# A decoder block on one core: the down projection with the tokens' operands as TensorE's weights

## The chip, the core and the metric

The kernel runs on one core of a Trainium2 chip. The metric is device microseconds per execution; the kernel before has a median of 1889.66 us over 3 runs (1889.62 to 1889.98). Five engines work side by side: TensorE (PE; its weight loads are shown apart as PEld), VectorE (DVE), ScalarE (ACT), GpSimd (POOL) and SyncE (SP), whose queue issues nearly all DMAs (SPq in the profile).

## The reference

One layer on 512 tokens of 2048 channels: RMSNorm, an input projection, three token mixers, an output projection with a residual, then a SwiGLU feed-forward layer of width 5632 with a second residual. The change concerns the last line, above all the product with `w_down`:

```python
x = x + mix @ w_out[l]
h2 = _rms_norm(x, norm2_g[l])
x = x + (jax.nn.silu(h2 @ w_gate[l]) * (h2 @ w_up[l])) @ w_down[l]
```

## The kernel before, in words

Arrays lie with channels on the 128 partitions and the 512 tokens on the free axis; the host turns the output back. Each fp32 operand is split into a high part rounded to fp32r and the rest (low part), and a product is three matmuls: high by high, high by low, low by high.

The stages in order: `in` (the first four tiles of the input projection, 16 steps k of 12 matmuls of 512 columns; lines 392 to 417), the other 26 tiles of the input projection with attention and convolution between them, the output projection, gate and up, and down. The rows of x and of w for the first steps are loaded by SP in the order of lines 288 to 292, ACT makes the high parts (`hh` L371, `wh` L245), DVE the low ones (`hl` L372, `wl` L232), and ten matmuls on a tile `idle` (L299) run ahead of the first one. `token_scale` sums squares over channels by matmuls with a column of ones (L322).

Gate/up and down use a Strassen-Winograd scheme: each block product is cut in 2 by 2 quarters and made of seven products q. The operands of the seven products are sums of quarters. For w these sums are made by POOL (`add` in `group`, L187); then ACT writes the high part twice, once to PSUM (`wn`, L251) and once to SBUF (`wh`, L252), and DVE subtracts to get the low part (`wl`, L232). `next_unit` hands out one such split unit of w at a time and splits two units ahead (`SPLIT_AHEAD`); three `wh` and three `wl` buffers exist. For the activations, ACT and DVE write tiles a (256 columns high, 256 low) in gate/up, which go to DRAM (`od`) and are loaded again in down.

Down in the kernel before: 25 blocks (table `DOWN`), each for two of the 16 tiles of 128 output channels and 5 to 8 of the 22 pairs of inner tiles. In `Block.multiply` (L1013) a 128x128 tile of w is TensorE's weights and the tokens move: `wh` by 512 columns (256 tokens high and low side by side), then `wl` by 256 columns (high alone). The sums have channels on partitions; unfinished ones go to DRAM (`yd`) and come back (`load_y`). `Down.done` adds PSUM to them on DVE (L1025, L1026; 128x256 each), the shared term u on POOL, and the residual x2 on POOL (L1147, L1148). `Down.store` writes 128x256 pieces to the output on SP (L1152), the last ones at once (`tail`).

Order is set by the program: `run(evacs)` issues what was put off ahead of each unit, `run(extras)` what was put off behind it; `later(n, ..., queue)` puts something off by n units. Each engine takes its instructions in that order, and SP takes DMAs in that order too.

Of the kernel before, what the change touches and what calls it, by code (L numbers as in the profile page):

```python
# [57 lines left out]
WARM = 10  # L58
# [12 lines left out]

GU_ORDER = [*range(1, 5), *range(6, NP), 0, 5]
STAY = (0, 5)


DOWN = [(0, 0, 5), (1, 0, 6), (2, 0, 7), (3, 1, 8), (4, 2, 9), (5, 3, 10), (6, 4, 11), (7, 5, 13),
        (0, 5, 12), (1, 6, 14), (2, 7, 15), (3, 8, 16), (4, 9, 17), (5, 10, 18), (6, 11, 19), (7, 13, 20),
        (0, 12, 17), (1, 14, 22), (2, 15, 22), (3, 16, 23), (4, 17, 24), (0, 17, 22), (5, 18, 25), (6, 19, 26), (7, 20, 27)]

FIRST = [min([w[1] for w in DOWN[t:]] + [99]) for t in range(len(DOWN) + 1)]  # L80
LAST = [max(w[2] for w in DOWN[:t + 1]) for t in range(len(DOWN))]
# [38 lines left out]
def kernel(ctx: ExitStack, tc: tile.TileContext, xT, wi, wo, wgu, wd, cst_in, outT):  # L120
# [27 lines left out]
    units = [wi[0][:, :T], wi[0][:, T:]] + [wi[u] for u in range(1, 2 * N_IN)]  # L148
# [19 lines left out]
    for u, unit in enumerate(units):  # L168
        entries.append((RAW_PLAIN[u % len(RAW_PLAIN)], u, [unit]))
        works.append((u, True, nc.vector))  # L170
# [33 lines left out]
    def down_block(n, half, first, end):  # L204

        parts = [(first, min(end, NP)), (0, end - NP)] if first < NP else [(first - NP, end - NP)]
        return [bass.AP(tensor=wd.tensor, offset=wd.offset + (n * P * NF + half * NP + a) * P,
                        ap=[[NF * P, P], [1, (b - a) * P]]) for a, b in parts if b > a]

    for t, (n, first, end) in enumerate(DOWN):  # L210
        group(f"d{t}", t % 2, (end - first) * P, {f"{i + 1}{k + 1}": down_block(n + 8 * i, k, first, end)
                                                  for i in range(2) for k in range(2)})
# [4 lines left out]
    def pump(limit):  # L217
        while at["entry"] < len(entries) and len(raws) < limit and entries[at["entry"]][0] not in held:
            buf, key, parts = entries[at["entry"]]
            t, o = take(buf, key, sum(p.shape[-1] for p in parts)), 0  # L220
# [15 lines left out]
    def split_up_to(i):  # L236
        while at["split"] <= min(i, len(works) - 1):
# [5 lines left out]
            if eng or "high" not in psum:  # L243
                eng = eng or nc.vector
                nc.scalar.copy(hi[:, :n], t[:, :n])  # L245
# [17 lines left out]
    def next_unit():  # L263
        sums_now()
        u = at["use"]
        at["use"] += 1
        lows_now()
        split_up_to(u + SPLIT_AHEAD)
        if not lows:
            pump(RAW_EARLY if u < 20 else RAW_BUFS)  # L270
        return splits.pop(u)
# [8 lines left out]
    nc.scalar.dma_start(cst, cst_in)  # L280
# [7 lines left out]
    for k in range(X_AHEAD):  # L288
        load_first(k)
        u = k if k < 2 else k // 2 + 1  # L290
        if u < RAW_EARLY and (k < 2 or k % 2 == 0):
            pump(u + 1)


    idle = slot("idle", BF16)
    nc.vector.memset(idle, 1.0)
    b = bank("idle")
    for i in range(WARM):
        nc.tensor.matmul(b, idle[:, :P], idle, start=True, stop=True)  # L299
# [10 lines left out]
    bones = cp.tile([P, 2], F32, name="bones")  # L310
    nc.vector.memset(bones, 0.0)
    nc.vector.memset(bones[0:HD, 0:1], 1.0)
    nc.vector.memset(bones[HD:P, 1:2], 1.0)
# [69 lines left out]
    def token_scale(acc, n, name, b=None):  # L383

        b = bank(name, NT) if b is None else b
        stat_rows(b[:, :, None], acc, ones)
        v, r = small(name + "v"), small(name + "r")
        nc.vector.tensor_scalar(v, b, 1.0 / n, EPS, op0=ALU.mult, op1=ALU.add)  # L388
# [5 lines left out]
    for k in range(2):  # L394
        h_hl[k] = scaled(xs[k], col(C_G1 + k), "h", k)
        split_up_to(k)
    pump(RAW_EARLY)
    add_square(ssum, xs[0], 0, "sq")
    for k in range(KT):

        if k == 0:
            h_hl[2] = scaled(xs[2], col(C_G1 + 2), "h", 2)
        if k < 2 or k % 2 == 0:
# [4 lines left out]
        if k and k + 2 < KT:  # L408
            h_hl[k + 2] = scaled(xs[k + 2], col(C_G1 + k + 2), "h", k + 2)
# [4 lines left out]
        h_lo.append(lo)  # L414
        for j in range(HEAD4):
            mm3(g4[j], wh[:, o:o + P], wl[:, o:o + P], hi, lo, k == 0, k == KT - 1)
            o += P
# [439 lines left out]
    x2d = {n: tc.dram_tile([P, T], F32, name=f"x2d{n}") for n in range(KT)}  # L857
# [15 lines left out]
    def scale_x2(n):  # L873
        j = n % NJ
        t = x2.pop(n)
        nc.sync.dma_start(x2d[n], t)
# [151 lines left out]
    class Wide(Block):  # L1028
# [55 lines left out]
        def piece(self, at, src):  # L1084
# [3 lines left out]
            for k in range(n):  # L1088
# [4 lines left out]
                if self.p in STAY:  # L1093
                    acts[q, self.p] = t
                if self.p not in STAY:
                    later(0, nc.sync.dma_start, od[self.p][:, (at + k) * T:(at + k + 1) * T], t.bitcast(F32),
                          queue=extras)
# [16 lines left out]
    y, yd = {}, {n: tc.dram_tile([P, T], F32, name=f"yd{n}") for n in range(KT)}  # L1114

    def visit(t):

        begin, last = [all(w[0] != DOWN[t][0] for w in part) for part in (DOWN[:t], DOWN[t + 1:])]

        return begin, last, t == 8 if DOWN[t][0] == 0 else last  # L1120

    def load_y(t):
        if t < len(DOWN):
            for n in (DOWN[t][0], DOWN[t][0] + 8):
                y[t, n] = slot(f"y{t}_{n}")
                if not visit(t)[0]:
                    nc.sync.dma_start(y[t, n], yd[n])
                if visit(t)[2]:
                    xr[n] = slot(f"yx{n}")
                    nc.sync.dma_start(xr[n], x2d[n])  # L1130

    class Down(Block):


        def __init__(self, t):
            super().__init__(f"d{t}", t % 2)
            self.n = DOWN[t][0]
            self.fresh, last, residual = visit(t)
            self.out = outT if last else yd
            self.tail = t == len(DOWN) - 1  # L1140
            self.y1, self.y2 = y.pop((t, self.n)), y.pop((t, self.n + 8))
            if residual:

                later(1, self.add_x2)

        def add_x2(self):
            nc.gpsimd.tensor_add(self.y2, self.y2, xr.pop(self.n + 8))  # L1147
            nc.gpsimd.tensor_add(self.y1, self.y1, xr.pop(self.n))  # L1148

        def store(self, n, t, cols):  # L1150
            def go():
                nc.sync.dma_start(self.out[n][:, cols], t[:, cols])  # L1152
            if self.tail:
                go()
            else:
                later(1, go, queue=extras)

        def done(self, q):
            one, two = slice(0, TH), slice(TH, T)
            if q == 1:  # L1160
                self.u = slot(f"{self.name}u")
                self.u1, self.u2 = halves(self.u)
                self.both(1, self.u1)
            elif q == 7:
                if self.fresh:
                    self.both(7, self.y2[:, two])
                else:
                    self.add(7, self.y2[:, two])
# [155 lines left out]
```

## Time and profile before

| | before |
|---|---|
| median of 3 runs | 1889.66 us (1889.62 to 1889.98) |
| the profiled execution | 1889.53 us, of it 1887.7 us span from the first to the last instruction |
| granted TensorE clock | 1.00 |
| PE busy; PEld busy | 1882.2 us; 1635.1 us |
| DVE, ACT, POOL busy | 1467.8, 1330.7, 996.4 us |
| DMA | 320.29 MB, mean 170 GB/s |

Busy time is the union of an engine's instructions. A matmul's own duration is longer than its distance to the next one, because matmuls are pipelined: how fast they go is read from the distance of their starts. A row of groups gives line, engine, operation, output<-inputs, shape, count, busy us, mean ns of one, and idle time ahead of it with what ended it. In a timeline the columns are start, duration, engine, line, operation, and in brackets the idle time before.

### The profile page before, as it was taken

How to read it: one execution, taken by the hardware profiler on the slowest of the kernel's cores; microseconds unless marked ns; L12 is line 12 of the kernel's file. 1: busy time of each engine (PE TensorE's matmuls, PEld its weight loads, DVE VectorE, ACT ScalarE, POOL GpSimd, SP SyncE). 2: the span in 40 equal slices, each digit the busy share in tenths (PEclk: the TensorE clock that was granted, in tenths of full speed). 3: DMA queues.
4: the chain of work that ended last, by engine and by line, in shares of the span. 5: the costliest groups of instructions: out<-in, count | busy, mean ns of one | idle time of the engine just before them, and what ended most of it. 6: DMA issues, size and time to landing. Idle time of an engine off the chain costs nothing.

```text
span 1887.7 us, 29650 instructions
## 1 busy us (share of the span) xinstructions
PE 1882.2 (100%) x10332; PEld 1635.1 (87%) x10332; DVE 1467.8 (78%) x2562; ACT 1330.7 (70%) x1856; POOL 996.4 (53%) x643
## 2 busy tenths in 40 slices
PE   9999999999999999999999999999999999999999
PEld 7888888888888888888888888888888888888888
DVE  6789978999679777777777777777787877677776
ACT  6356645453467887888888888888878877676775
POOL 0111011010003887877878878788767656565775
PEclk9999999999999999999999999999999999999999
DMA  7242242343343444454544545445447878777885
GB/s 269 86 126 86 81 123 88 112 118 122 124 144 105 142 147 153 139 181 152 164 144 146 177 141 167 140 160 167 146 159 248 272 261 275 256 260 232 306 272 196
DMA packets 136311, 320.29 MB, mean 170 GB/s; under 512 B 15585, under 2 KB 31073, under 8 KB 136161
## 3 DMA queue, kind: packets, MB, share of 16 engines
q1 hardware_dynamic: 136016, 318.31, 52.4%
q8 instruction: 81, 1.33, 0.3%
q14 instruction: 70, 0.57, 0.1%
q10 hardware_dynamic: 144, 0.10, 0.0%
HBM read 254.11 MB, written 55.84 MB: 164 GB/s over the span
## 4 chain that ended last, share of the span: by engine, by line
PE 99%; DMA 0%; SPq 0%; ACT 0%; DVE 0%; issue 0%; ACTq 0%; DVEq 0%
PE out L1013 68%; PE o L276 3%; PE o L274 3%; PE o L275 3%; PE cq L276 2%; PE cq L274 2%; PE cq L275 2%; PE av L274 1%; PE ak L274 1%; PE aq L274 1%; PE aq L276 1%; PE av L276 1%; PE ak L276 1%; PE av L275 1%; PE aq L275 1%; PE ak L275 1%
## 5 line engine op out<-in xcount | busy, mean ns | idle before, releaser
L1013 PE MATMUL out<-h,wh 128*128 128x512 f32 x2464 | 588.5, 391 | 0.0
L1013 PEld LDWEIGHTS out<-h,wh 128*128 128x128 f32 x2464 | 452.7, 188 | 87.5
L1013 PEld LDWEIGHTS out<-h,wl 128*128 128x128 f32 x2464 | 315.9, 191 | 12.0
L1013 PE MATMUL out<-h,wl 128*128 128x256 f32 x2464 | 319.6, 283 | 0.0
L1013 PE MATMUL out<-a,wh 128*128 128x512 f32 x1232 | 296.2, 391 | 0.0
L1013 PEld LDWEIGHTS out<-a,wh 128*128 128x128 f32 x1232 | 225.7, 188 | 43.5 <-ACT wh L252 0.4
L245 ACT CAST wh<-w 128x1024 fp32r<-128x1024 f32 (+1 forms) x93 | 96.8, 1041 | 122.4 <-PE o L275 51.6
L1013 PEld LDWEIGHTS out<-a,wl 128*128 128x128 f32 x1232 | 159.4, 191 | 6.9
L1013 PE MATMUL out<-a,wl 128*128 128x256 f32 x1232 | 161.5, 283 | 0.0
L232 DVE TENSOR_TENSOR wl<-w,wh 128x1024 fp32r<-128x1024 f32 (+1 forms) x93 | 112.5, 1209 | 39.4 <-ACT wh L245 39.3
L466 DVE SCALAR_TENSOR_TENSOR y<-bu,cst,y 128x511 f32<-128x511 f32 (+14 forms) x120 | 87.6, 730 | 0.4
L1025 DVE TENSOR_TENSOR y<-y,out 128x256 f32<-128x256 f32 x93 | 39.1, 421 | 46.0 <-PE out L1013 44.4
L274 PE MATMUL o<-mh_c,wh 128*128 128x512 f32 x128 | 51.1, 399 | 0.0
L274 PE MATMUL cq<-hh,wh 128*128 128x512 f32 x128 | 51.1, 399 | 0.0
L276 PE MATMUL cq<-hh,wl 128*128 128x512 f32 x128 | 50.0, 391 | 0.0
L276 PE MATMUL o<-mh_c,wl 128*128 128x512 f32 x128 | 50.0, 391 | 0.0
L275 PE MATMUL cq<-hl,wh 128*128 128x512 f32 x128 | 50.0, 390 | 0.0
L275 PE MATMUL o<-ml_c,wh 128*128 128x512 f32 x128 | 49.9, 390 | 0.0
L1026 DVE TENSOR_TENSOR y<-y,out 128x256 f32<-128x256 f32 x101 | 42.5, 421 | 3.5
L389 POOL TENSOR_TENSOR lvr<-lvv,nhalf 128x4 f32<-128x4 f32 x1 | 1.9, 1927 | 73.3 <-DVE lvv L388 73.3
L187 POOL TENSOR_TENSOR w('s', 'g1')_5687<-w('21', 'g1')_5533,w('22', 'g1')_5531 128x1024 f32<-128x1024 f32 x1 | 2.5, 2451 | 69.8 <-DVE wl L232 69.8
L868 DVE TENSOR_TENSOR xr<-xr,o 128x512 f32<-128x512 f32 x32 | 21.9, 683 | 13.6 <-PE o L276 12.8
(3137 smaller groups left out, 4868.9 us busy)
## 6 DMA issues: line engine op xcount, KB each, us to landing
a<-od SPq DMA_DIRECT2D x175, 256.0 KB, 5.0
od<-a SPq DMA_DIRECT2D x147, 256.0 KB, 4.6
w<-in_wi SPq DMA_DIRECT2D x59, 512.0 KB, 3.7
w<-in_wo SPq DMA_DIRECT2D x32, 512.0 KB, 3.6
yd<-y SPq DMA_DIRECT2D x68, 128.0 KB, 4.7
y<-yd SPq DMA_DIRECT2D x34, 256.0 KB, 4.8
x<-in_xT SPq DMA_DIRECT2D x16, 256.0 KB, 7.7
xr<-in_xT SPq DMA_DIRECT2D x16, 256.0 KB, 3.9
```

Of the source, the lines that this page charges most:

```text
L187: eng.tensor_add(out[:, :n], raws[key[a]][0][:, :n], raws[key[b]][0][:, :n])
L232: fn(*args)
L245: nc.scalar.copy(hi[:, :n], t[:, :n])
L274: nc.tensor.matmul(out, wh, xh, start=start, stop=False)
L275: nc.tensor.matmul(out, wh, xl, start=False, stop=False)
L276: nc.tensor.matmul(out, wl, xh, start=False, stop=stop)
L389: nc.gpsimd.tensor_tensor(r, v, nhalf[:, :NT], op=ALU.pow)
L466: nc.vector.scalar_tensor_tensor(yconv[j][:, i:], hconv[j][:, :T - i], c, yconv[j][:, i:], op0=ALU.mult, op1=ALU.add)
L868: nc.vector.tensor_add(t, t, b)
L1013: nc.tensor.matmul(out, lhs[:, s], rhs, start=begin, stop=x is xs[-1] and low == flip[0], skip_group_check=True)
L1025: sign(out, out if first is None else first, main)
L1026: sign(out, out, rest)
```

## The change

**Down.** The 16 sums of 128 tokens by 512 channels (key `(g, i, k, a)`: channel half i and 512 of its channels g, token half k and 128 of its tokens a) stay in SBUF from start to end, and start as x2. Down becomes 12 visits (`DOWN`): six ranges of pairs, 4, 3, 4, 3, 4 and 4 long, each for both g. A visit does the seven products in the order `D_ORDER`; a product has two units of w (A with two pairs, B with two or one, four channel tiles each) and two banks, one for each a. The tokens' tile (128 high or 128 low columns) is TensorE's weights, 512 columns of w move:

```diff
-                    out, lhs, rhs = (b[:, TH:], wl, x[:, :TH]) if low else (b, wh, x)
-                    nc.tensor.matmul(out, lhs[:, s], rhs, start=begin, ...
+        def multiply(self, q, b, units, a, lo, hi, start, stop):
+            high, low = slice(a * P, (a + 1) * P), slice(TH + a * P, TH + (a + 1) * P)
...
+                    nc.tensor.matmul(b[:, lo:hi], x[:, high], wh[:, s], start=start, ...
+                    nc.tensor.matmul(b[:, lo:hi], x[:, high], wl[:, s], start=False, ...
+                    nc.tensor.matmul(b[:, lo:hi], x[:, low], wh[:, s], start=False, ...
```

The split (`eng == "moves"`) copies with the tiles of a unit reordered, and the sums of w are four per unit kind on POOL: 21+11 (four units ahead), 21+22, +11, +12. A quarter of w is loaded in rows of 1 KB (two pairs) or 512 bytes (one).

```diff
+        for i, c in enumerate("AB"):
+            sums[base - 4 + i].append(add(c, "11", buf=bufs[c]["s"]))
+            sums[base + i].append(add(c, "22"))
+            sums[base + 3 + i].append(add(c, "11", last=True))
+            sums[base + 7 + i].append(add(c, "12"))
...
+                nc.scalar.copy(by(near), src)
+                nc.scalar.copy(by(hi), src)
+                nc.vector.tensor_sub(by(lo), src, by(near).bitcast(F32))
```

PSUM is added to the sums by `done`, mostly by DVE with 128x512 adds; q=1 goes by an ACT copy `u` to POOL:

```diff
+                if q == 7:
+                    self.add(1, 0, a, b, by)
+                    self.add(1, 1, a, b, by)
+                elif q == 1:
+                    nc.scalar.copy(self.u[a], b)
+                    later(a, self.add, 0, 0, a, self.u[a], nc.gpsimd)
+                elif q == 5:
+                    self.add(0, 1, a, b, by)
+                    self.add(1, 1, a, b, by, "tensor_sub")
+                elif q == 6:
+                    by.tensor_add(self.u[a], self.u[a], b)
...
```

behind q=6, six POOL adds of u follow in each visit.

**Turning.** x2 is read back in blocks of 32 by 32 during gate/up (from the fourth pair on, one key each), turned by a DVE transpose and stored as `x2t`. At the end `store` turns a sum and writes it with four DMAs of 32x16 runs of 32 floats:

```diff
+    def store(key, lo=0, hi=T, engs=(nc.sync,), now=False):
+        nc.vector.transpose(z[:, lo:hi], y[key][:, lo:hi])
+        def go():
+            for part in range(4):
+                to = out[c + lo:c + hi, 256 * k + P * a + 32 * part:256 * k + P * a + 32 * part + 32]
+                engs[part % len(engs)].dma_start(to.rearrange("(b i) t -> i b t", i=32), ...
+        if now:
+            go()
+        else:
+            later(1, go, queue=extras)
```

The eight sums of g=1 are stored during the last visit, one per unit. Of g=0, keys (1,1) and (1,0) are stored through `later` behind q=4 and q=2; (0,0) and (0,1) in the last product with `now=True`. That last product does a=0, then a=1 in two halves of 256 columns, and does not call `run(extras)`:

```diff
+            if tail:
+                for n, (a, lo, hi) in enumerate(((0, 0, T), (1, 0, TH), (1, TH, T))):
+                    self.multiply(q, out[n], units, a, lo, hi, True, True)
+                    nc.vector.tensor_add(s, s, out[n][:, lo:hi])
+                    store(key, lo, hi, (nc.sync, nc.scalar), now=True)
+                    if n == 0:
+                        for b in range(2):
+                            store(self.sum(0, 0, b), now=True)
+                return
```

**Loads.** `load_next` loads the activations' tiles and the sums one or two per unit, at most `FEED` = 46 tiles ahead; no pair stays in SBUF from gate/up, which now takes its pairs in plain order.

**The start.** The first 512 columns of w are two loads and two units; `idle` is 128 wide and has 8 matmuls; the constants' first 16 columns are loaded alone; DVE makes the first `wh`; step 0 does both units' `wh` by `hh` first, then the rest; from there `scaled` for step k+2 stands ahead of `next_unit`.

```diff
+            for part, u in ((0, 0), (0, 1), (2, 0), (1, 0), (1, 1), (2, 1)):
+                for j in range(2):
+                    w = first[u][part == 2][:, j * P:(j + 1) * P]
+                    nc.tensor.matmul(g4[2 * u + j], w, (hi, lo, hi)[part], start=part == 0, stop=False)
```

**token_scale**, where no bank is given (two places), transposes the squares' sums on TensorE and lets DVE reduce them, in place of the matmuls with ones.

Three places show how the instructions move. First TensorE in the middle of a product of down: `a_17` is the tile of pair 17, `wh`/`wl` a unit's high and low part, `out` a PSUM bank. Before:

```order
L1013 MATMUL out_5948<-a_17_17592,wh_17889 128x512
L1013 MATMUL out_5948<-a_18_17798,wh_17889 128x512
L1013 MATMUL out_5948<-a_11_16378,wl_17890 128x256
L1013 MATMUL out_5948<-a_12_16380,wl_17890 128x256
L1013 MATMUL out_5948<-a_13_16770,wl_17890 128x256
```

After (lines of the changed kernel):

```order
L1310 MATMUL out_5942<-wh_16513,a_8_16042 128x512
L1311 MATMUL out_5942<-wl_16514,a_8_16042 128x512
L1312 MATMUL out_5942<-wh_16513,a_8_16042 128x512
L1310 MATMUL out_5941<-wh_16535,a_9_16071 128x512
L1311 MATMUL out_5941<-wl_16536,a_9_16071 128x512
L1312 MATMUL out_5941<-wh_16535,a_9_16071 128x512
```

The 256-column matmuls are gone, w is what moves, and a unit's `wl` is read by its second matmul; in the blocks before, the products took turns in beginning with `wh` or with `wl`. Second, VectorE over the first three products of a block; `y` are sums, `wl` the low parts, `d12` a block or visit. Before:

```order
L1025 TENSOR_TENSOR y_11_17057<-y_11_17057,out_5949 128x256
L1026 TENSOR_TENSOR y_11_17057<-y_11_17057,out_5949 128x256
L232 TENSOR_TENSOR wl_17391<-w('11', 'd12')_17218,wn_17392 128x1024
L1025 TENSOR_TENSOR y_3_17055<-y_3_17055,out_5950 128x256
L1026 TENSOR_TENSOR y_3_17055<-y_3_17055,out_5950 128x256
L232 TENSOR_TENSOR wl_17419<-w('21', 'd12')_17105,wn_17420 128x1024
```

After, in a visit of three pairs:

```order
L1320 TENSOR_TENSOR y_15052<-y_15052,out2_5943 128x512
L1320 TENSOR_TENSOR y_15087<-y_15087,out2_5943 128x512
L1320 TENSOR_TENSOR y_15054<-y_15054,out3_5944 128x512
L1320 TENSOR_TENSOR y_15089<-y_15089,out3_5944 128x512
L285 TENSOR_TENSOR wl449_16300<-w('21', 'd3A')_16057,wn449_16301 128x1024
L285 TENSOR_TENSOR wl450_16321<-w('21', 'd3B')_16101,wn450_16322 128x512
L285 TENSOR_TENSOR wl451_16342<-w('21', 'd3A')_16057,wn451_16343 128x1024
```

Four adds of 512 columns now stand ahead of a unit's `wl`; between `wl449` and `wl451` POOL adds 11 to 21 in place. Third, SP's DMAs at the end of the program: `out_T` is the output, `zo` a turned sum. Before:

```order
L1152 DMA out_T<-y_6_19400 128x256
L1152 DMA out_T<-y_15_19606 128x256
L1152 DMA out_T<-y_7_19602 128x256
L1152 DMA out_T<-y_15_19606 128x256
L1152 DMA out_T<-y_7_19602 128x256
```

After:

```order
L252 DMA w('12', 'd11A')_18844<-in_wd 128x4x256
L1252 DMA out_T<-zo 32x16x32 x4
L252 DMA w('12', 'd11B')_18875<-in_wd 128x4x256
L1252 DMA out_T<-zo 32x16x32 x34
L1252 DMA out_T<-zo 32x8x32 x4
L1252 DMA out_T<-zo 32x16x32 x16
```

The last 16 rows, the stores of (1,1) and (1,0), stand behind the four half-size ones (32x8x32) that wait for the very last matmuls; of the 34, the last ten belong to the last product. Another six of the end stand on ACT's queue.

More of the change, by code (lines that the diff above doesn't have):

```diff
@@ L69 @@
 NP = NF // 2
[L72 to L81, printed above, removed]
+FEED = 46
+GU_ORDER = [*range(NP)]
+D_ORDER = (7, 1, 5, 6, 4, 2, 3)
+RANGES = ((0, 4), (4, 7), (7, 11), (11, 14), (14, 18), (18, 22))
+DOWN = [((r + g) % 2, r) for r in range(len(RANGES)) for g in range(2)]
 LAID = (5, 7, 6, 4, 3, 1, 2)
@@ L202 @@
                                              for i in range(2) for k in range(2)})
[L204 to L212, printed above, removed]
+    bufs = {"A": dict(zip(("21", "11", "s", "22"), ("21a", "22a", "sa", "22b"))),
+            "B": dict(zip(("21", "11", "s", "22"), ("21b", "11", "12", "sb")))}
@@ L214, with pump @@
     splits = {}
     at = {"entry": 0, "split": 0, "use": 0}
-    def pump(limit):
-        while at["entry"] < len(entries) and len(raws) < limit and entries[at["entry"]][0] not in held:
+    def pump(limit, most=99):
+        while at["entry"] < len(entries) and len(raws) < limit and entries[at["entry"]][0] not in held and most:
+            most -= 1
             buf, key, parts = entries[at["entry"]]
+            if len(parts[0].shape) == 3:
+                n = 4 * parts[0].shape[-1]
+                nc.sync.dma_start(take(buf, key, n)[:, :n].rearrange("p (n f) -> p n f", n=4), parts[0])
+                at["entry"] += 1
+                continue
@@ L289 @@
         load_first(k)
[L290 to L295, printed above, removed]
+        if k < 4 or k % 2 == 0:
+            pump(k + 2 if k < 4 else k // 2 + 4)
+    idle = slot("idle", BF16, P)
     nc.vector.memset(idle, 1.0)
@@ L298 @@
     for i in range(WARM):
-        nc.tensor.matmul(b, idle[:, :P], idle, start=True, stop=True)
+        nc.tensor.matmul(b, idle, idle[:, None, :].to_broadcast([P, NT, P]), start=True, stop=True)
     b = idle = None
@@ L1111, in piece4 @@
             self.l = self.r = None
[L1114 to L1130, printed above, removed]
@@ L1193, in load_act @@
-    def load_act(q, pairs):
-        for j in pairs:
-            if j in STAY:
-                continue
-            acts[q, j] = slot(f"a{q}_{j}", F32R)
-            at = LAID.index(q)
-            nc.sync.dma_start(acts[q, j].bitcast(F32), od[j % NP][:, at * T:(at + 1) * T])
-    blk = gate = None
-    for g in range(2 * NP + len(DOWN)):
-        t = g - 2 * NP
-        if t < 0:
-            p, m = GU_ORDER[g // 2], g % 2
-            blk = Wide(p, m, gate if m else None)
-            gate = blk if m == 0 else None
-        else:
-            n, first, end = DOWN[t]
-            blk = Down(t)
+    y = {}
@@ new lines, with turn_x2, turn_x2_now @@
+    turns = {}
+    def turn_x2(key):
+        z = turns[key] = slot("z")
+        for part in range(4):
+            nc.sync.dma_start(by_blocks(z, part), turned(x2d, key, part))
+    def turn_x2_now(key):
+        t = slot("zt")
+        nc.vector.transpose(t, turns.pop(key))
+        later(1, nc.sync.dma_start, x2t[key], t, queue=extras)
+    feed = []
+    for key in D_ORDER:
+        feed += [(key, j) for j in range(*RANGES[0][:2])]
+        feed += [n for n in SUMS if n[0] == DOWN[0][0] and n[1] == (key == 7)] if key in (1, 7) else []
@@ L1211 @@
+    blk = gate = None
+    for g in range(2 * NP):
+        p, m = GU_ORDER[g // 2], g % 2
+        blk = Wide(p, m, gate if m else None)
+        gate = blk if m == 0 else None
         for i, q in enumerate(ORDER):
@@ L1239 @@
+    blk = gate = None
+    for t in range(len(DOWN)):
+        blk = Down(t)
+        for k, q in enumerate(D_ORDER):
+            blk.product(k, q)
     while evacs or extras:
```

271 lines of the change are left out of this document (170 added, 101 removed).

## Prediction

> **What bounds the kernel now.** I read the page first.
>
> ```profile
> span 1887.7 us, 29650 instructions
> ...
> PE 1882.2 (100%) x10332; PEld 1635.1 (87%) x10332; DVE 1467.8 (78%) x2562; ACT 1330.7 (70%) x1856; POOL 996.4 (53%) x643
> ...
> PE 99%; DMA 0%; SPq 0%; ACT 0%; DVE 0%; issue 0%; ACTq 0%; DVEq 0%
> ```
>
> The chain of waits is TensorE for 99% of the span. So a time can only come from fewer or quicker matmuls, from the few microseconds ahead of the first and behind the last one, or from new waits. The windows of the down stage (PE, PEld, DVE, ACT, POOL busy, each with its instructions; clock; DMA share; GB/s) show that it runs without a gap:
>
> ```profile
> 1500.00:1600.00 100.00, 100.00 (x576) 88.32 (x575) 72.03 (x106) 70.48 (x81) 58.72 (x33) 1.00 0.77 258
> 1600.00:1700.00 100.00, 100.00 (x576) 88.38 (x575) 70.44 (x104) 70.18 (x73) 60.71 (x37) 1.00 0.79 264
> ```
>
> 576 matmuls per 100 us, half of 512 and half of 256 columns. The groups give their number, the timeline the distances:
>
> ```profile
> L1013 PE MATMUL out<-a,wh 128*128 128x512 f32 x1232 | 296.2, 391 | 0.0
> L1013 PE MATMUL out<-a,wl 128*128 128x256 f32 x1232 | 161.5, 283 | 0.0
> ```
>
> ```profile
> 1604.68 3.82 PE L1013 MATMUL out<-a,wh 128*128 128x512 f32 x16
> 1608.33 2.08 PE L1013 MATMUL out<-a,wl 128*128 128x256 f32 x16
> 1610.25 2.00 PE L1013 MATMUL out<-a,wh 128*128 128x512 f32 x8
> ```
>
> Sixteen of 512 take 3.65 us, 228 ns each; sixteen of 256 take 1.92 us, 120 ns each. Half the columns cost more than half the time: a line through the two puts about 12 ns on each matmul, whatever its width. Down is 2464 matmuls at 100/576 us: 427.8 us.
>
> **Down's matmuls.** The same 946176 columns go through in 1836 matmuls of 512 and 24 of 256 (the last product). The trace has 512-column matmuls alone in the output projection, first and last of 19 rows in order of time:
>
> ```profile
> 479.83 0.39 PE L276 MATMUL o<-mh_c,wl 128*128 128x512 f32 x1
> ...
> 483.91 0.39 PE L276 MATMUL o<-mh_c,wl 128*128 128x512 f32 x1
> ```
>
> 18 distances in 4.08 us: 226.7 ns. 1836 x 0.2267 + 24 x 0.120 = 419.1 us, **8.7 us less**; at 228 ns it is 6.3 less. Below 6 or above 10 nothing in these rows reaches. The Trainium skill, "TensorE: Matmul & The Clock Gate", section Back-to-back issue gap, gives an isolated gap of N/2.4 + 2.5 ns, 216 and 109 ns here; by it the saving would be an estimated 1.6 us, since it puts only 2.5 ns on a matmul. The rows above have 228 and 120, so the row's figure stands in the sum.
>
> **The start.** PE's first real matmul waits for a chain of loads and casts:
>
> ```profile
> 4.02 0.72 ACT L371 ACTIVATE hh<-x,cst 128x512 fp32r<-128x512 f32 x1 [1.36 <-DMA cst<-in_cst]
> 4.65 0.60 ACT L245 CAST wh<-w 128x512 fp32r<-128x512 f32 x1
> 5.33 0.59 PE L274 MATMUL in<-hh,wh 128*128 128x512 f32 x1
> ...
> 14.02 0.39 PE L274 MATMUL in<-hh,wh 128*128 128x512 f32 x1
> 14.78 0.50 PE L275 MATMUL in<-hl,wh 128*128 128x512 f32 x1 [0.37 <-DVE hl L372]
> ```
>
> The high part of w no longer stands behind `hh` on ACT: DVE makes it, half as wide, while ACT makes `hh`. The first matmul can then start at the end of `hh`, near 4.7: 0.6 us. Step 0 takes four `wh` by `hh` matmuls first, which covers a wait of about 0.2 us for the low parts. The hole at 14.02 to 14.78, 0.53 us beyond one distance, comes from a late `hl`, whose `scaled` now stands ahead of the split: gone. **1.3 us less**, between 0.5 (only the hole goes) and 2. The eight warm matmuls are hidden either way, as PE waits for the cast. In `token_scale`, eight matmuls with ones become four transposes:
>
> ```profile
> 50.23 0.79 PE n L322 x8
> ...
> 53.90 0.44 PE r1s L328 x4
> ```
>
> ```profile
> 51.30 1.31 POOL L389 TENSOR_TENSOR n1r<-n1v,nhalf 128x4 f32<-128x4 f32 x1 [49.19 <-DVE n1v L388]
> ```
>
> 0.35 us less at each of two places, **0.7 us**. DVE's reduce, some 0.7 us, comes ahead of POOL's power; POOL is done at 52.6 now and the spread stands at 53.9, which is cover for it. Without the cover it would cost the 0.35 again: 0 to 0.7.
>
> **Turning x2.** In gate/up, 16 keys each add a DVE transpose, four loads and a store to a pair's two blocks (224 matmuls at the 576 per 100 us of above, 39 us). Their cover is SP's and DVE's idle time there, since no engine but PE is on the chain; I take zero, up to 1 us if a load of w that is queued behind them on SP comes late. VectorE's sums for the first gate block (L187) fall where DVE is full; zero to 1 us as well: they are issued four units of w ahead of their use.
>
> **The other engines in down.** Their prices:
>
> ```profile
> 1427.23 1.02 ACT L251 CAST wn<-w('s', 'g5')_14540 128x1024 fp32r<-128x1024 f32 x1 [1.46 <-DVE wl L232]
> 1428.18 1.05 ACT L252 CAST wh<-w('s', 'g5')_14540 128x1024 fp32r<-128x1024 f32 x1
> 1434.18 2.42 POOL L187 TENSOR_TENSOR w('s', 'u5')_14744<-w('s', 'u5')_14744,w('11', 'u5')_14657 128x1024 f32<-128x1024 f32 x1
> 1436.34 1.21 DVE L232 TENSOR_TENSOR wl<-w('21', 'u5')_14555,wn 128x1024 fp32r<-128x1024 f32 x1
> L868 DVE TENSOR_TENSOR xr<-xr,o 128x512 f32<-128x512 f32 x32 | 21.9, 683 | 13.6 <-PE o L276 12.8 <-DMA xr<-in_xT 0.8
> L792 ACT CAST mh_c<-mix_c 128x512 fp32r<-128x512 f32 x8 | 4.6, 616 | 0.0
> L1148 POOL TENSOR_TENSOR y<-y,yx 128x512 f32<-128x512 f32 x8 | 10.4, 1301 | 0.0
> ```
>
> A visit of four pairs is 168 matmuls, 38.1 us. In it DVE does 14 low parts and 16 adds (14 x 1.21 + 16 x 0.683 = 27.9 us), ACT 28 casts and two copies (30.2), POOL eight sums and eight adds (8 x 2.42 + 8 x 1.30 = 29.8). A visit of three pairs has 28.6 us for 24.1, 24.1 and 25.3 us (units B at half width, 0.6 to 0.7 an operation on DVE and ACT, 1.3 on POOL). All fit, with 84 to 88% there. But one chain does not, in a visit of three pairs. Units A take 2.72 us there, B 1.36. When q=7 ends (4.08 us into the visit), DVE adds four times (2.8 us with gaps), then makes the low part of 21+22 (1.2): about 8.3. Only then may POOL add 11 in place (2.4): 10.7; then ACT `wn` and `wh` (2.1): 12.8. PE wants this unit at 12.24. Behind that POOL add stand the same one for B and two adds of u, behind ACT's casts those of B, and they have room. I expect a wait of 0.75 us with the hand-overs, in each of the four visits of three pairs: **3 us more**. In visits of four pairs PE wants it at 16.3 and it is there at 14. From below: zero, if the hand-overs are quicker than that; from above 7, if the visits of q=5 and the first visit, where the last gate/up pieces still occupy ACT and POOL, lose as much. For the loads I see no loss: DMA has a share of 0.79 now, and yd's traffic goes.
>
> **The end.** Before, the last matmul ends at 1884.06 and the last instruction at 1887.7: 3.6 us.
>
> ```profile
> 1883.07 0.99 PE L1013 MATMUL out<-a,wl 128*128 128x256 f32 x7
> ...
> 1884.63 0.42 DVE L1026 TENSOR_TENSOR y<-y,out 128x256 f32<-128x256 f32 x1
> 1885.08 0.33 SPq L1152 DMA_DIRECT2D out_T<-y  x1
> ```
>
> After: count from the start of the last product, which takes PE 5.6 us. Its first 12 matmuls end at 2.9; add and transpose (0.69 each; a transpose has no row, and 128x512 work on DVE has 0.4 to 0.7) give the first store at 4.35. From there SP has 30 DMAs and ACT 6: in amount 32 of 512 runs of 128 bytes. The 16 of keys (1,1) and (1,0) were ready long before, but stand on SP behind the halves that DVE turns last, at 7.4. Nothing else is left to hide them. Their price: SP's issue, and the packets. The output's stores, and two windows in which the queue moved one DMA alone (1 us with 128 packets of 1 KB, 1.4 us with 128 of 2 KB, each with 16 small ones for its end):
>
> ```profile
> L1152 SPq DMA_DIRECT2D out_T<-y x12: 332/338/430, 1846.0 to 1885.1; - x12
> DMA to landing us min/median/max: 1.7/2.2/5.3
> ```
>
> ```profile
> q1 hardware_dynamic: 144, 0.13, 39.4%
> ```
>
> ```profile
> q1 hardware_dynamic: 144, 0.26, 50.2%
> ```
>
> 39.4% of 16 engines for 1 us is 6.30 us, 50.2% of 1.4 us is 11.24: the 131 KB between them cost 4.94 us, 0.0377 ns a byte, and 1.36 us or 9.4 ns a packet remain. A packet of 128 bytes is thus an estimated 14.2 ns, a DMA of 512 of them on 16 engines 0.455 us, and 32 take 14.6 us. The end: 4.35 + 14.6 + 2.2 for landing = 21.1, which is 15.5 behind PE instead of 3.6: **11.9 us more**. From below: if packets cost nothing beyond SP's 30 issues at 0.34 us, 4.35 + 10.2 + 2.2 = 16.75, 7.5 more. From above: if a packet costs what the 1 KB window's mean is, 43.8 ns, the 32 take 44.8 us and the end is 42 us longer. I take the line through the two windows, as the size lies close to its fixed part.
>
> **Sum.** 1889.5 (profiled; the median of the runs is 1889.66, so the same) - 8.7 - 1.3 - 0.7 + 3 + 11.9 = **1893.7 us**. The measurement tells about 0.2% from no change, 3.8 us here; the forecast is just beyond, on the slow side.
>
> **Rivals.**
>
> *The end is paid by issue, and no wait in down.* -8.7 - 1.3 - 0.7 + 7.5 = 1886.3; with a start 0.7 better, 1885.6. It decides where a DMA of 512 runs takes less than 0.34 us. For it: PE has no wait in down now, and the measured stores wait mostly for SP. Against: the windows' 9.4 ns a packet. 0.24, a good half of it faster by over 0.2%.
>
> *A short run costs double.* At 28.4 ns a packet the 32 DMAs take 29 us, the end is 26.4 us longer, and the time is 1908. No window above has data packets under 1 KB. The Trainium skill, "DMA: Bandwidth & Descriptors", Specifications, says that under 512 bytes the DMA does a read-modify-write, which speaks against this change; no run here shows it yet. 0.12.
>
> *A full engine.* If each of the 28 products in visits of three pairs waits 0.4 us, since DVE, ACT and POOL stand at 84 to 88% there and hand over to one another, down costs 11 us, not 3: 1902. For it: three engines in one chain; against: units are split two ahead. 0.07.
>
> *Time goes with columns.* If PE's 12 ns a matmul belong to something other than its number, the 8.7 us stay: 1902. Against it stand the 226.7 ns. 0.05.
>
> **How the numbers follow.** The forecast has 0.52, with its own range 1889 to 1898 (waits 0 to 5 us, packets 11 to 18 ns); a third of it, 0.18, is within 0.2%. Faster by over 0.2%: 0.13 of the first rival. Within 0.2%: 0.18 of the forecast and the first rival's other 0.11, 0.29. Slower: the other 0.34 of the forecast and 0.12 + 0.07 + 0.05 from the rest, 0.58. The range takes in the first rival and most of the doubled packet: 1885.5 to 1906; the 42 us of the upper bound are left out, as the line excludes them.
>
> **What would show it.** In the changed profile: starts of down's matmuls 227 ns apart; the first real matmul near 4.7; waits of PE on ACT `wh` (L284) of 0.5 to 1 us in visits d2, d3, d6 and d7 and none elsewhere; a last matmul near 1876 and 15 us of transposes and DMAs behind it, the 16 last issued in a row on SP. Wrong I am if the last matmul is no earlier than 1882 (the waits or the columns), or if the end is under 10 us or over 22 (the packets).

## The result, and the profile after

The changed kernel takes 1904.81 us (median of 5 runs, 1902.93 to 1905.37) against 1889.66 for the kernel before: a ratio of 1.0079, with a 95% interval of 1.0068 to 1.009. The forecast was 1893.7 with a range up to 1906.0: the sign is right, the time is inside the range, and three quarters of the loss were not foreseen. That the time lies inside is partly luck: the forecast's own range was 1889 to 1898, and the range reached to 1906 for the rival of short runs at a double price, which the runs below do not show. The profiled execution took 1905.0 us, its span is 1903.1.

The page of the changed kernel, its span, engines and chain of waits:

```profile
span 1903.1 us, 28403 instructions
...
PE 1874.6 (99%) x9718; PEld 1603.6 (84%) x9718; DVE 1466.9 (77%) x2472; ACT 1347.0 (71%) x1869; POOL 1057.3 (56%) x662
...
PE 96%; DVE 1%; POOL 1%; DMA 1%; issue 0%; ACT 0%; SPq 0%; DVEq 0%; POOLq 0%
```

TensorE has 614 matmuls less and 7.6 us less of busy time, and the kernel is longer all the same: its share of the chain fell from 99% to 96%. The stages of the two profiles, each from the start of its first matmul to the start of the next stage's:

| part | before, us | after, us | difference |
|---|---|---|---|
| to the start of gate/up | 596.2 | 595.0 | -1.2 |
| gate/up | 858.7 | 862.4 | +3.8 |
| down, to the end of the last matmul | 429.2 | 421.0 | -8.2 |
| from there to the end of the span | 3.7 | 24.7 | +21.0 |
| span | 1887.7 | 1903.1 | +15.4 |

(Counted to the end of its last matmul, as in an expectation below, gate/up before is 858.8.)

**Down is quicker, as forecast.** The timeline at its start, and the window that was shown of before (PE, PEld, DVE, ACT, POOL busy with instructions; clock; DMA share; GB/s):

```profile
1457.43 0.39 PE L1310 MATMUL out<-wh,a 128*128 128x512 f32 x1
1457.66 0.39 PE L1311 MATMUL out<-wl,a 128*128 128x512 f32 x1
1457.89 0.39 PE L1312 MATMUL out<-wh,a 128*128 128x512 f32 x1
```

```profile
1500.00:1600.00 100.00, 99.95 (x439) 81.98 (x439) 74.74 (x95) 75.73 (x93) 81.14 (x50) 1.00 0.67 228
```

Starts are 0.23 us apart. 439 matmuls of 512 columns fill 100 us, 227.8 ns each, the waits in that window included.

**Gate/up has a new wait.** The waits of PE over the whole span (engine, line, releaser: us in total, times, longest):

```profile
PE out L1076 <- DVE n2v L433: 2.0, 1, 2.0
...
PE in L318 <- ACT wh L289: 0.4, 1, 0.4
PE out L1311 <- DVE wl L285: 0.4, 1, 0.4
```

The first row stands in the first gate block. What DVE does there:

```profile
601.61 1.22 DVE L267 TENSOR_TENSOR wl<-w('21', 'g0')_5527,wn 128x1024 fp32r<-128x1024 f32 x1
602.74 1.22 DVE L184 TENSOR_TENSOR w('s', 'g0')_5681<-w('s', 'g0')_5681,w('11', 'g0')_5581 128x1024 f32<-128x1024 f32 x1
605.04 1.22 DVE L267 TENSOR_TENSOR wl<-w('s', 'g0')_5681,wn 128x1024 fp32r<-128x1024 f32 x1 [1.08 <-ACT wn L295]
606.18 0.15 DVE L433 TENSOR_SCALAR n2v<-out 128x4 f32<-128x4 f32 x1
```

The sum of w (L184) now stands on DVE, ACT's cast waits for it, DVE waits 1.08 us for that cast, and only then reads the four sums of norm 2 (`n2v`) out of the bank that PE wants next. Before, `n2v` came at 605.05, with a stage that began 1.2 us later. What the wait costs is more than its 2.0 us. Windows of PE from the wait on (here the numbers of PE alone matter, and the clock behind POOL's):

```profile
604.00:606.30 2.30, 0.42 (x4) 0.22 (x2) 1.26 (x2) 2.30 (x3) 0.00 (x0) 1.00 0.49 134
606.30:608.00 1.70, 1.61 (x8) 1.61 (x9) 1.68 (x3) 1.70 (x3) 1.58 (x1) 0.59 0.32 128
608.00:610.00 2.00, 2.00 (x7) 1.61 (x7) 1.97 (x4) 1.77 (x2) 2.00 (x2) 0.50 0.00 0
610.00:612.00 2.00, 2.00 (x13) 1.65 (x12) 1.97 (x4) 0.53 (x2) 1.92 (x2) 1.00 0.61 236
```

Behind a gap of 2.25 us between the starts of two matmuls the granted clock is 0.5 until 610: matmuls of 256 columns stand 0.213 us apart, not 0.12, and those of 512 stand 0.427 apart, not 0.228.

How much of the 3.8 us belongs to the clock, three of the runs below tell: they have the same wait, and the clock stays at 1.00 behind it. The run with four DMAs for a sum is one. Its first row is the first matmul behind the wait; eight matmuls take 1.05 us from there to the next row, and 1.72 in the changed kernel, from 606.39 to 608.11.

```profile
606.09 1.22 PE L1076 MATMUL out<-h,wl 128*128 128x256 f32 x8 [1.97 <-DVE n2v L433]
607.14 2.00 PE L1076 MATMUL out<-h,wh 128*128 128x512 f32 x8
```

```profile
606.30:608.00 1.70, 1.70 (x12) 1.57 (x12) 1.70 (x3) 1.70 (x3) 1.70 (x1) 1.00 0.10 41
```

Gate/up takes 861.1 us in these three, and 862.4 to 862.5 in the four traces in which the clock falls. So the wait costs 2.4 us and the lower clock 1.4 more, where it comes; an expectation below puts them at 2.0 and 1.8.

**The end is 24.7 us.** The output's stores in the last 27 us (duration of an issue min/median/max in ns, first and last start), how long a DMA takes to land, and what SP waited for in the last 48 us:

```profile
L1252 SPq DMA_DIRECT2D out_T<-zo x38: 315/502/551, 1879.6 to 1900.2; - x38
...
DMA to landing us min/median/max: 1.6/2.0/2.8
```

```profile
SPq L1252 <- DMA out_T<-zo: 16.4, 4, 15.1
```

The last three stretches of issues, of SP and of ACT:

```profile
1859.93 4.46 SPq L1252 DMA_DIRECT2D out_T<-zo  x8
...
1877.16 3.88 ACTq L1252 DMA_DIRECT2D out_T<-zo  x6
...
1879.58 21.11 SPq L1252 DMA_DIRECT2D out_T<-zo  x38
```

SP issues one DMA each 0.556 us (21.11 / 38), and 38 stand behind the last matmul, not 30: eight belong to sums of the visit before, transposed by 1862.3. SP stood still from 1864.4 to 1879.58 with those eight ready. 15.1 us of this it waited for another DMA. Which one, the built program tells. Its rows name the completion counters that each DMA waits for; SP's, and ACT's six:

```
903 L1252 DMA out_T<-zo 32x16x32 [waits DMAHW0_49]
904 L1252 DMA out_T<-zo 32x16x32 [waits DMAHW2_49,DVE_49]
905 L1252 DMA out_T<-zo 32x16x32 [waits DMAHW4_49]
906 L1252 DMA out_T<-zo 32x16x32 [waits DMAHW7_49]
907 L1252 DMA out_T<-zo 32x16x32 [waits DMAHW2_49]
908 L1252 DMA out_T<-zo 32x16x32 [waits DMAHW3_49,DVE_49]
...
1807 L1252 DMA out_T<-zo 32x16x32 [waits DMAHW1_49,DVE_49]
1808 L1252 DMA out_T<-zo 32x16x32 [waits DMAHW3_49]
1809 L1252 DMA out_T<-zo 32x8x32 [waits DMAHW5_49,DVE_49]
1810 L1252 DMA out_T<-zo 32x8x32 [waits DMAHW6_49]
1811 L1252 DMA out_T<-zo 32x8x32 [waits DMAHW0_49,DVE_49]
1812 L1252 DMA out_T<-zo 32x8x32 [waits DMAHW1_49]
```

There are eight counters, 0 to 7, dealt in one sequence to the DMAs of both engines, and a DMA waits until the one that had its counter before has landed. From 904 on SP's row leaves out 1, 3, 5, 6, 0 and 1: these are ACT's six, which were dealt in there. So SP's 908, a store that was ready at 1860.5, waits for counter 3 of ACT's second store, which ACT can issue only within the last product, at 1877.55.

### The profile page after: what moved, and what is told of

It reads as the page before. It is cut to its first block, busy times and chain, and to the rows that moved or that the text cites. A ratio compares the mean times of both kernels' runs of the same rounds, so it can differ in the third digit from the quotient of the medians.

```text
span 1903.1 us, 28403 instructions
## 1 busy us (share of the span) xinstructions
PE 1874.6 (99%) x9718; PEld 1603.6 (84%) x9718; DVE 1466.9 (77%) x2472; ACT 1347.0 (71%) x1869; POOL 1057.3 (56%) x662
## 4 chain that ended last, share of the span: by engine, by line
PE 96%; DVE 1%; POOL 1%; DMA 1%; issue 0%; ACT 0%; SPq 0%; DVEq 0%; POOLq 0%
PE out L1076 45%; PE out L1311 7%; PE out L1312 7%; PE out L1310 7%; PE o L318 3%; PE o L319 3%; PE o L320 3%; PE cq L320 2%; PE cq L318 2%; PE cq L319 2%; PE av L318 1%; PE ak L318 1%; PE av L320 1%; PE aq L320 1%; PE aq L318 1%; PE ak L320 1%
## 5 line engine op out<-in xcount | busy, mean ns | idle before, releaser
L1076 PEld LDWEIGHTS out<-h,wl 128*128 128x128 f32 x2464 | 316.6, 192 | 14.2 <-DVE n2v L433 2.2
L1311 PE MATMUL out<-wl,a 128*128 128x512 f32 x620 | 241.1, 389 | 0.4 <-DVE wl L285 0.4
L1312 PE MATMUL out<-wh,a 128*128 128x512 f32 x620 | 240.4, 388 | 0.0
L1310 PE MATMUL out<-wh,a 128*128 128x512 f32 x620 | 240.4, 388 | 0.0
L289 ACT CAST wh<-w 128x1024 fp32r<-128x1024 f32 (+2 forms) x94 | 96.7, 1030 | 123.4 <-PE o L319 54.6
L267 DVE TENSOR_TENSOR wl<-w,wh 128x1024 fp32r<-128x1024 f32 (+2 forms) x95 | 112.8, 1187 | 37.2 <-ACT wh L289 37.0
L1311 PEld LDWEIGHTS out<-wl,a 128*128 128x128 f32 x620 | 116.4, 188 | 26.3 <-DVE wl L285 2.5
L1310 PEld LDWEIGHTS out<-wh,a 128*128 128x128 f32 x620 | 116.4, 188 | 24.2
L1312 PEld LDWEIGHTS out<-wh,a 128*128 128x128 f32 x620 | 116.4, 188 | 23.5
L1320 DVE TENSOR_TENSOR y<-y,out 128x512 f32<-128x512 f32 x164 | 106.3, 684 | 32.9 <-PE out L1312 20.8
```

Source lines behind the costliest of these rows:

```text
L267: fn(*args)
L289: (nc.vector.tensor_copy if u == 0 else nc.scalar.copy)(hi[:, :n], t[:, :n])
L1076: nc.tensor.matmul(out, lhs[:, s], rhs, start=begin, stop=x is xs[-1] and low == flip[0], skip_group_check=True)
L1310: nc.tensor.matmul(b[:, lo:hi], x[:, high], wh[:, s], start=start, stop=False, skip_group_check=True)
L1311: nc.tensor.matmul(b[:, lo:hi], x[:, high], wl[:, s], start=False, stop=False, skip_group_check=True)
L1312: nc.tensor.matmul(b[:, lo:hi], x[:, low], wh[:, s], start=False, stop=last, skip_group_check=True)
```

## The experiments

Times are medians; ratios are to the kernel before (1889.36 to 1889.53 us beside these runs), with 95% intervals. "Tail" is the time from the end of down's last matmul to the end of the span.

### No store on ACT

```
-                    store(key, lo, hi, (nc.sync, nc.scalar), now=True)
+                    store(key, lo, hi, now=True)
```

> The changed kernel, but the last stores (the halves that DVE turns last) are all issued on SP; none is left on ACT. Theory (a completion counter shared by the two queues): in the changed kernel SP stands still for 15.1 us, from 1864.4 to 1879.58, before the store of a sum that was turned at 1859.83, since its counter is also that of a store that ACT issues at 1877.55. Without stores on ACT SP has no such wait: the eight stores left over go out by 1869, the last 36 (28 of 512 runs at 0.55 us, 8 of 256 at some 0.35) take 18.2 us from 1877.1, and 2.4 us follow as now: a tail of 19 us behind the last matmul instead of 24.65, the time near 1899.5. Rival (issue alone sets the end, no counter): six more DMAs on SP, 2 to 3 us slower than the changed kernel, 1907 to 1908. Rival (packets alone set the end): the same bytes, 1904.8.

1900.21 us, ratio 1.0053 (1.0039 to 1.0066). Six more DMAs on SP, and 4.6 us less. The wait for a DMA in the last visit is gone; SP's only long wait there is for the sums themselves. Its last issues, and that wait:

```profile
1877.09 19.23 SPq L1252 DMA_DIRECT2D out_T<-zo  x36
```

```profile
SPq L1252 <- DVE zo L1245: 9.1, 2, 8.7
```

36 DMAs in 19.23 us are 0.534 each; the tail is 20.4 us. The shared counter cost 4.6 us net, and both rivals fall.

### The first gate block's sums on GpSimd

```
-                eng = nc.vector if name == "g0" else nc.gpsimd
+                eng = nc.gpsimd
```

> The changed kernel, but GpSimd makes the sums of w for the first gate block too, as it does for all others. Theory: DVE's sum (1.22 us at 602.74) and the low part behind it delay n2v to 606.18; PE waits 2.0 us for it and then has half the clock until 610.2, which costs 1.8 us more; both go: 1904.8 - 3.8 = 1901.0, gate/up 858.8 us as before. Rival (the wait alone, the lower clock is a coincidence): 1902.8. Rival (GpSimd takes 2.42 us a sum and hands the unit over later, so the wait only changes its place): 1904 to 1905.

1901.33 us, ratio 1.0062 (1.0049 to 1.0074): 3.5 us less. Gate/up takes 858.7 us, as before the change. DVE comes to `n2v` at 603.26, and in the windows PE has neither the wait nor the lower clock:

```profile
603.26 0.15 DVE L433 TENSOR_SCALAR n2v<-out 128x4 f32<-128x4 f32 x1
```

```profile
604.00:606.30 2.30, 2.30 (x15) 2.00 (x14) 2.23 (x5) 2.15 (x3) 2.30 (x2) 1.00 0.04 11
606.30:608.00 1.70, 1.70 (x11) 1.44 (x10) 1.70 (x3) 0.86 (x2) 1.70 (x2) 1.00 0.16 14
```

So one DVE sum in the wrong place cost all of the 3.8 us of the profiled execution: 2.4 by the wait, 1.4 by the clock. That the lower clock follows the wait is shown by its absence here; that it need not follow, by the three traces named above. It shows also that turning x2, which stays in this run, costs TensorE nothing.

### One DMA for a sum, or four of long rows

The last step of the turning, by blocks, is left out in both: rows of 2 KB leave SBUF as they lie, and the output does not stand in the layer's order. The first has one DMA for a sum, the second four of 32 rows, all on SP.

```
-                engs[part % len(engs)].dma_start(to.rearrange("(b i) t -> i b t", i=32),
-                                                 z[32 * part:32 * part + 32, lo:hi].rearrange("p (b j) -> p b j", j=32))
+                engs[part % len(engs)].dma_start(outT[n][r, lo:hi], z[r, lo:hi])
```

> The changed kernel, but each sum is stored by one DMA, as it lies in SBUF, in 128 rows of 2 KB, on SP (the last transposition of the output, by blocks, is left out: the output does not stand in its order). DVE's transposes stay. Theory (the end is paid by SP's issue of many DMAs of short runs, and the counter): nine DMAs at 0.34 us are left behind the last product; the last half is turned at 1879.9, five issues take 1.7 us, 2.4 us follow: a tail of 5.6 us, the time 1885.8. Rival (DVE's transposes or the adds hold the end): the tail stays over 10 us and the time over 1890.

> As the run with one DMA for a sum, but four DMAs of 32 rows of 2 KB for each, all on SP: the number of DMAs of the changed kernel, without its short runs (the output does not stand in its order). Theory (each DMA costs SP its issue, 0.34 us where a run is long, 0.5 to 0.55 where there are 512 short ones): 36 x 0.34 = 12.2 us from 1877.1 and 2.4 us: a tail of 13 us, the time 1893.5. Rival (only the 512 short runs cost, the number of DMAs does not): as with one DMA, 1886. Rival (only the number of DMAs costs): as with all stores on SP, a tail of 19 us, 1899.5.

1885.24 us (0.9979, 0.997 to 0.9988) and 1897.33 us (1.0042, 1.003 to 1.0055); the tails are 7.0 and 17.9 us. One row for each: the issues behind the last product.

```profile
L1250 SPq DMA_DIRECT2D out_T<-zo x9: 332/333/454, 1877.1 to 1881.7; - x9
```

```profile
L1252 SPq DMA_DIRECT2D out_T<-zo x36: 315/422/438, 1876.0 to 1892.6; - x36
```

The first came out near its expectation (time 1885.8, tail 5.6). The second lies 3.8 us above its expectation: a DMA of 32 long rows does not cost the 0.34 us of a single issue when 36 stand in a row, but 0.47 from start to start (16.6 us / 35). So from 20.35 us of tail (all on SP) the 16 times longer runs take away 2.4, and the four times smaller number of DMAs 10.9 more. The number of DMAs is most of the price, the shortness of their runs the small part.

### The early sums ahead of the last product's

All on SP; the 16 DMAs of the sums (1,1) and (1,0) are put on the queue before the last product, not after it.

```
                 out = banks + outs[:1]
+                while extras:
+                    run(extras)
```

> As the run with all stores on SP, but the 16 DMAs of the four sums (1,1) and (1,0), turned by 1873.3, stand on SP ahead of the last product's, not behind them. Theory (SP's issue, 0.52 us a DMA in a row, sets the end): the 16 go out from 1870.4 to 1879, where SP stood idle for 8.7 us; 20 are left, 10.3 us, to 1889.2, and 2.4 us follow: a tail of 13 us behind the last matmul, the time 1893.2. Rival (only the number of DMAs in flight or of packets on the DMA engines, 13.2 ns each, sets the end): 36 x 512 / 16 x 13.2 ns = 15.2 us from 1870.4, a tail of 9 to 10 us, 1889.5. Rival (order is no matter, the whole output must be written after the last product anyhow): 1900.2.

1893.82 us, ratio 1.0023 (1.0014 to 1.0032), where 1893.2 was expected: 6.4 us less than with all stores on SP alone, and 11 less than the changed kernel. SP's row of issues now begins at 1870.35.

### Two queues

As above, and the four DMAs of a sum alternate between SP and ACT in the whole last visit; then the same with GpSimd's sums for the first gate block.

```
-    def store(key, lo=0, hi=T, engs=(nc.sync,), now=False):
+    def store(key, lo=0, hi=T, engs=(nc.sync, nc.scalar), now=False):
```

> As the run before, but the four DMAs of each sum go by turns to SP and ACT, in the whole last visit. Theory (each engine pays the issue of its own DMAs): ten DMAs of the last product on each queue, 5.2 us from 1877.1, and 2.4 us follow: a span of 1885 to 1886, as the packets of 36 DMAs at 13.2 ns take until 1885.6; the time 1887. Rival (both queues share one issuer, so a DMA on ACT costs what it costs on SP): 1893. Rival (ACT's issue among its casts makes PE wait in the last visit): the last matmul ends later than 1879.5.

> The run before, with GpSimd making the sums of w for the first gate block too: the best version that the runs so far point to. Theory: the two gains add, 1887 - 3.6 = 1883.4, faster than the kernel before by 0.3%. Rival (the last product's end is bound by the DMA engines or a shared issuer): 1889 to 1890, no change.

1892.47 us (1.0011, 1.0002 to 1.002) and 1888.56 us (0.9995, 0.9986 to 1.0004). The second queue gains 1.4 us where 6 were expected. It does issue at the same time, and no product waits; but now the DMA engines are full. Windows of the run with two queues, and of the one with SP alone (their sixth number is the clock, the seventh DMA's share):

```profile
1871.00:1885.00 14.00, 5.18 (x35) 4.57 (x33) 6.09 (x11) 0.21 (x1) 1.66 (x2) 0.77 1.00 140
```

```profile
1878.30:1890.00 11.70, 0.04 (x1) 0.00 (x0) 1.41 (x4) 0.00 (x0) 0.00 (x0) 0.59 0.71 110
```

With SP alone the engines are busy for 0.71 of the time and SP's issue is the bound. With two queues the share is 1.00 and the packets are the bound, 8040 and 7614 of them in 14 us on 16 engines: 14.2 ns each. The profiled execution of this run (1889.95) is 2.5 us shorter than the median of its runs. It is one in which the clock did not fall in gate/up, which is worth 1.4; the rest is left open. The gate block's gain adds, 3.9 us, and the whole is no different from the kernel before.

### Down's products in halves

Each matmul of 512 columns is issued as two of 256, with the same weights.

```
+                    for n in ((lo, lo + TH), (lo + TH, hi)) if hi - lo == T else ((lo, hi),):
+                        s, o = slice(f * T + n[0], f * T + n[1]), b[:, n[0]:n[1]]
```

> The changed kernel, but each of down's 1836 matmuls of 512 columns is issued as two of 256, with the same weights and the same result. Theory (some 12 to 13 ns belong to each matmul, whatever its width): 1836 x (2 x 120 - 226.7) ns = 24.4 us more, less the 1 to 2 us of waits in down that the longer products cover: 1927 to 1929. Rival (time goes with columns, and down was shorter for another reason): 1904.8.

1926.32 us, ratio 1.0195 (1.0181 to 1.0209): 21.5 us more than the changed kernel. Down takes 443.7 us, 22.7 more. That is near the expected 24.4 less the 1.6 us of waits that the changed kernel has in down (see below) and this run does not have.

```profile
1500.00:1600.00 100.00, 100.00 (x836) 100.00 (x835) 70.82 (x90) 72.52 (x91) 76.00 (x48) 1.00 0.67 221
```

836 matmuls of 256 columns in 100 us are 119.6 ns each, the prediction's 120. The price that belongs to a matmul's number is shown, and time by columns alone falls. Each half comes with a weight load of its own (PEld has as many instructions as PE and is busy throughout), so these runs do not tell whether the price is the matmul's or its load's.

### The last four sums turned by TensorE

GpSimd's sums for the first gate block, the early sums ahead, and for the last four sums 16 transposes of TensorE, a copy, and one DMA of runs of 512 bytes each (two for the last):

```
+                    for o in range(lo, hi, P):
+                        nc.tensor.transpose(b[:, o:o + P], y[key][:, o:o + P], ident)
+                    copy(z[:, lo:hi], b[:, lo:hi])
+                    nc.sync.dma_start(outT.rearrange("n p t -> (n p) t")[c + lo:c + hi, t:t + P].rearrange("(b i) t -> i b t", i=P),
+                                      z[:, lo:hi].rearrange("p (b t) -> p b t", t=P))
```

> The changed kernel with GpSimd's sums for the first gate block, the 16 DMAs of the sums (1,1) and (1,0) on SP ahead of the last product's, and the last four sums turned in another way: TensorE transposes their blocks of 128 columns (16 transposes of some 0.11 us), ScalarE or VectorE copies them to SBUF, and one DMA of runs of 512 bytes (two of half the size for the last) stores each. Theory (the end is paid by the number of DMAs behind the last product): SP is done with the 16 at 1874, five DMAs are left where 20 stood, the last matmul of down ends near 1874.5 with the eight transposes that stand between its products, the last DMA is issued near 1877, 2.8 us follow: a span of 1880 and a time of 1882, faster than the kernel before by 0.4%. Rival (landing of strided stores or the DMA engines hold the end, whatever their number): 1888, as with two queues.

1883.71 us, ratio 0.9971 (0.9959 to 0.9982): faster than both kernels, 5.7 us than the one before and 21 than the changed one. The timeline of the end:

```profile
1872.57 1.04 PE L1298 MATMUL zp<-ident,y 128*128 128x128 f32 x8
...
1874.87 0.82 PE L1298 MATMUL zp<-ident,y 128*128 128x128 f32 x6
...
1875.72 3.25 SPq L1300 DMA_DIRECT2D out_T<-zf  x5
1876.14 0.44 PE L1298 MATMUL zp<-ident,y 128*128 128x128 f32 x2 [0.46 <-DVE zf L1299]
```

Eight transposes between the parts of the last product cost TensorE 1 us, and five DMAs stand where 20 stood; the tail is 6.9 us. The last issue ends at 1879.0, 2 us later than expected, as these DMAs take SP 0.45 to 0.76 us. The number of DMAs, the length of their runs and the engine that turns change together in this run; it does not tell their parts.

### The start alone

The kernel before, with the change's start and its `token_scale` only.

> The kernel before, with the change's start and its token_scale alone (halved first loads of w, DVE's first cast, the order of step 0, eight warm matmuls, four transposes and a reduce where eight matmuls with ones stood). By the prediction 1.3 + 0.7 = 2.0 us less, 1887.6. By the profiles of the changed kernel and its variants, in which the output projection ends at 594.4 to 595.2 where it ended at 596.3: 1.1 to 1.9 less, 1887.7 to 1888.5. Rival (what the start gives is lost to later waits on ACT's casts): 1889.6.

1887.84 us, ratio 0.9992 (0.9983 to 1.0001): 1.5 us less, by medians; the interval reaches from 3.2 less to 0.2 more. Its profile has the end of the output projection 1.7 us earlier than before and its first real matmul at 4.49, with no hole behind it:

```profile
4.49 2.06 PE L431 MATMUL in<-hh,wh 128*128 128x512 f32 x3
```

## Why the prediction was right, and where not

**Down's matmuls, -8.7: right.** Starts of 227 ns, and the halves show the price by number. Down without its waits takes 419.4 us (421.0 - 1.6), where 419.1 was forecast; the 427.8 for the kernel before, from the count in a window, stands 1.4 under its trace. The Trainium skill's 2.5 ns on a matmul ("TensorE: Matmul & The Clock Gate", Back-to-back issue gap) would have given an estimated 1.5 us of saving (604 matmuls fewer; the prediction says 1.6). Down as a whole lost 8.2, and the measurement decides.

**The start and token_scale, -2.0: near.** 1.5 measured alone, 1.2 in the changed kernel. The first matmul stands at 4.59 where 4.7 was forecast; in the changed kernel a later wait for ACT's cast (L289, in the list of PE's waits) gives 0.4 back.

**Turning x2, 0: right.** Gate/up is 858.7 us with it and without, once the sums are on GpSimd.

**The first gate block's sums, "zero to 1 us": wrong, 3.8.** The step that failed is "they are issued four units of w ahead of their use". That is true of w, but the late one was not w: it was `n2v`, which stands behind the sum in DVE's order, and a bank of PE's hangs on it. What stands behind the added instruction on its own engine was not looked at. The lower clock behind the wait, 1.4 of the 3.8, was no part of the sum either.

**Waits in down, +3: too high, 1.6.** The list of PE's waits has 0.4 us in down, but it counts only what lies behind a matmul's full duration. The row of the weight loads shows six waits:

```profile
PEld out L1311 <- DVE wl L285: 2.5, 6, 0.8
```

By the distances of PE's starts beyond 227 ns the six cost 1.6 us: 0.13 to 0.24 each in the four visits of three pairs, 0.33 and 0.62 in the two visits of four pairs that follow them (d4 and d8). The unit that the prediction names came in time. In the first visit of three pairs (from 1533.6) DVE's adds and low part hold POOL, and ACT waits for POOL.

```profile
1540.95 2.40 POOL L229 TENSOR_TENSOR w('21', 'd2A')_15735<-w('21', 'd2A')_15735,w('11', 'd2A')_15783 128x1024 f32<-128x1024 f32 x1 [8.70 <-DVE wl L285]
...
1543.38 1.02 ACT L283 CAST wn<-w('21', 'd2A')_15735 128x1024 fp32r<-128x1024 f32 x1 [0.84 <-POOL w('21', 'd2A')_15735 L229]
1544.34 1.05 ACT L284 CAST wh<-w('21', 'd2A')_15735 128x1024 fp32r<-128x1024 f32 x1
...
1548.89 1.22 DVE L285 TENSOR_TENSOR wl<-w('22', 'd2A')_15879,wn 128x1024 fp32r<-128x1024 f32 x1
```

ACT's `wh` ends at 1545.39, 11.8 us into the visit. The forecast was 12.8, and PE wants the unit at 12.24. The four adds take 2.48 us, not 2.8, and the hand-overs next to nothing. What came late was DVE's low part of the next product, which stands behind four more adds: it ends at 1550.11, and PE's matmul with it starts at 1550.16. So the links named in the prediction leave out DVE's low part, the last one ahead of PE.

**The end, +11.9: stores in a row behind the last product, as forecast, but at a wrong price, 21.0.** The prediction lets the packets set the pace, "in amount 32 of 512 runs" at 0.455 us each. The end is over the 22 us at which it says that it is wrong in the packets, and it is, in two ways. With the stores on SP the packets are not what bounds the end: they take 13 ns each (forecast 14.2), while SP needs 0.53 to 0.56 us for a DMA. The lower bound's 0.34 us for an issue came from single stores, between which SP had time. And SP could not start at 4.35: the counter shared with ACT held it until 1879.58 and pushed eight more DMAs behind the last product, 4.6 us net. The counter was no part of the sum.

**The rivals.** "The end is paid by issue, and no wait in down" was right that the issue sets the pace and wrong in its price, 0.34 us for 0.53 to 0.56; its 1886 missed by more than the forecast did. "A short run costs double" falls: 13 ns, and 16 times longer runs save only 2.4 us. That its 1908 lies nearest to the measured time is chance. The Trainium skill, "DMA: Bandwidth & Descriptors", Specifications, speaks of a read-modify-write below 512 bytes; in these runs a run of 128 bytes shows no double cost. "A full engine" falls with the waits (six, 1.6 us, where it has 28 and 11), "time goes with columns" with the halves.

So the sign came from the right term, and the sum was 11 us short: 9.1 in the end, 3.8 in gate/up and 0.8 in the start, less 2.5 in down, where 1.4 of the waits did not come and the rest is the kernel before.

## What to carry to other kernels

Count what is left to issue behind the last product, by the time a DMA takes in a row and not by that of a single one, and look at which stores share a completion counter: a ready store can wait for one that another engine issues at the very end. When a sum moves to a busy engine, ask first what small operation stands behind it there, and whether a bank of TensorE hangs on that. The turning itself was worth its while only where the last sums left in few DMAs.

## What the hardware showed that was not expected

- A wait of about 2 us (2.24 to 2.25 us from start to start) stands in the first gate block of seven traces. In four (the changed kernel, no store on ACT, one DMA for a sum, the early sums) TensorE's granted clock fell to 0.5 behind it, for 3.41 us each time; in three (four DMAs, two queues, halves) it did not. In all traces the clock changes a whole number of 3.41 us steps behind its first row. Counted in these steps, at least 2.0 us of the gap lie within one step in the four traces, and at most 1.7 in the three. So the same wait costs 2.4 or 3.8 us, by where it falls; this is read from seven traces, and no run moved the wait on purpose. The Trainium skill, "TensorE: Matmul & The Clock Gate", Part 1: The HAM clock gate, puts the lower clock behind at least one idle window of about 3.4 us. Here 2.0 us within a step were enough.
- The issue of such a store on SP takes 0.32 to 0.33 us alone, and in a row 0.42 for 32 rows of 2 KB or 0.50 for 512 runs of 128 bytes; from start to start that is 0.47 and 0.53 to 0.56.
- Two queues fill the 16 DMA engines with runs of 128 bytes at 140 GB/s (share 1.00); with SP's queue alone the end runs at 110 to 115 and a share of 0.71 to 0.75.
